# Holding DMA additions into weights back behind the first norm's factors and the constants

## The chip, the cores and the metric

The kernel runs on one core of a Trainium2 chip. The metric is the time of one execution on the device in microseconds (us). Before the change it was run three times: 941.42, 941.53 and 942.64 us, with a median of 941.53 us. One further execution was profiled. All durations of single instructions below come from that one.

## The reference

The model is an encoder trunk of two layers on 256 tokens with 1024 features each. Everything is float32. A layer has three parts, each with a norm ahead of it:

```python
for l in range(DEPTH):                                   # 2 layers
    x = x + 0.5 * swiglu(rms_norm(x, ffn1_norm[l]), ffn1_w_gate[l], ffn1_w_up[l], ffn1_w_down[l])
    h = rms_norm(x, mix_norm[l])
    proj = h @ w_in[l]                                   # queries, keys and values of two kinds of attention
    ...
    x = x + concat(out_a, out_b) @ w_out[l]
    x = x + 0.5 * swiglu(rms_norm(x, ffn2_norm[l]), ffn2_w_gate[l], ffn2_w_up[l], ffn2_w_down[l])
return rms_norm(x, final_norm)

rms_norm(x, g) = x * rsqrt(mean(x * x) + 1e-6) * g
swiglu(h, ...) = (silu(h @ w_gate) * (h @ w_up)) @ w_down     # hidden width 2816
```

So there are four feed-forward blocks (ffn) and two mixers, six norms ahead of them and a last one. All weights come from the chip's main memory, once.

## The kernel before

**Products.** Each float32 operand is split in two parts: ACT casts it to the matmul's rounded type (`act.copy`), and DVE subtracts that from the original. A product is then three matmuls: high by high, low by high, high by low. For a weight this means that a raw tile is loaded by DMA, and each half of it (j = 0, 1) costs one ACT cast and one DVE subtraction of 128x1024, which write two tiles (hi and lo) that PE reads.

**The list of weights.** `specs` is a list of steps in the order of use. An ffn has six column groups: group 0 is specs 0 to 3 (gate and up, two halves of the 1024 input features each), group 1 is specs 4 to 9 (four for gate and up, two for the down projection of the group before). In groups 2, 3 and 4 (`SEVEN`) the four block products of gate and up are made out of seven products in place of eight. This needs sums of weight blocks, and `seven()` makes them. It loads four raw tiles, here a, b, d and c; for group 2 they are specs 10, 11, 12 and 13. Two of the sums are made by the DMA engines: a DMA on POOL's queue that adds a block of w_up, read from main memory, onto a raw tile that already lies on the chip (`accum_op=ALU.add`). This is a "DMA addition". One adds block c onto raw tile b as soon as b's own load has been issued (`behind`). The other adds block b onto raw tile a once a has been split (`prep`). There are two such additions in each of three groups of four ffns, 24 in all. The remaining sums are DVE additions (`plus`).

**The planner.** `ahead(n)` runs while the program is written, not on the chip. It emits loads (on SP's queue), preparations and splits in the order of the list, as far as the number of raw tiles (`N_RAW` = 6) and the lookahead allow. A spec's split n is 2 * spec + j. It is called at each use of a weight (`weights()`), and where the second half of a weight is first read (`Split.part`).

**Holding back.** `issue(add)` appends a DMA addition to `pending`, and emits it at once unless `hold[0]` is true. `flush()` sets `hold[0]` to false and emits what is pending. `hold[0]` is set to true near the end of each ffn (`ffn_end`) and at the mixer's output projection. `Norm.stats()` flushes.

**The norms.** A norm's square sums are made by ACT. `stats()` (line 381) then sums them on DVE (`ms`), raises them to the power -1/2 on POOL (`r`), flushes, and halves r on DVE (`hr`). The factor r isn't multiplied into the activations: ACT's SiLU reads a finished gate product from PSUM with r as its scale (`tmp<-ps,r`), and DVE multiplies the up product by hr (`s<-ps,hr,tmp`), which gives the hidden tile. PE later transposes that tile (`ps<-ident,s`) for the down projection.

**The first stage.** `take_x` takes in x and the first weights by hand. `take_x(0)` and `take_x(1)` transpose x and split specs 0 and 1; between the calls PE makes the products of the first 512 features. `take_x(2)` (line 442) finishes the first two splits, which drops their raw tiles, calls `ahead(7)`, takes the last squares, calls `stats()`, and then `constants()` (line 469). `constants()` puts on POOL: eight small DMAs (gains, sink logits, the vectors of lambda), an iota, twelve memsets, four copies, a negation, and two products of lambda's vectors. Behind it PE makes the second half of gate and the second half of up, 24 matmuls each, and then starts on group 1's gate.

**Banks and order.** PSUM has eight banks. The ffn's output takes four; gate and up of one group take the other four, so the next group's gate writes into banks that the SiLUs of this one read first. Outside the middle of the mixer, each engine runs its instructions in the order in which the program gives them (`keep_in_program_order`); between engines, semaphores order them. An engine runs its own list strictly in that order: what stands behind a waiting instruction waits too. POOL's list holds both its own arithmetic and the issue of its DMAs. In the middle of the mixer a scheduler orders the instructions by times that it works out.

Of the kernel before, what the change touches and what calls it, by code (L numbers as in the profile page):

```python
# [34 lines left out]
def trunk(ctx: ExitStack, tc: tile.TileContext, x, n1, g1, u1, d1, nm, w_in, sink,  # L35
# [44 lines left out]
    def tmp(tag="tmp", bufs=5, shape=(P, 2, 256), dt=F32):  # L80
        return tp.tile(list(shape), dt, tag=tag, bufs=bufs, name=nm_(tag))
# [76 lines left out]
            issue(s.behind)  # L158


    pending, hold = [], [False]

    def issue(add):
        pending.append(add)
# [3 lines left out]
    def flush():  # L168
        hold[0] = False
        while pending:  # L170
            pending.pop(0)()
# [53 lines left out]
    def ahead(n):  # L225

        n = min(n, 2 * len(specs) - 1)
        while True:
            if at["split"] <= n and at["prep"] > at["split"] // 2:
                for _ in emit_split(*divmod(at["split"], 2)):  # L230
                    pass
                at["split"] += 1
            elif at["prep"] <= min(n // 2 + 1, len(specs) - 1) and at["dma"] > at["prep"] and \
                    (specs[at["prep"]].prep is None or at["split"] >= 2 * at["prep"]):
                if specs[at["prep"]].prep is not None:
                    specs[at["prep"]].prep()
                at["prep"] += 1
            elif at["dma"] < min(at["use"] + AHEAD, len(specs)) and (specs[at["dma"]].moves is None or len(raws) < N_RAW):
                if specs[at["dma"]].moves is not None:
                    for _ in emit_dma(at["dma"]):  # L240
                        pass
                at["dma"] += 1
            else:
                break
# [58 lines left out]
    class Norm:  # L303
# [77 lines left out]
        def stats(self, n=512):  # L381
            ms = tmp("ms", 2, (P, 2))
            dve.tensor_reduce(ms, self.ss.rearrange("p t (h q) -> p t h q", q=n // 256)[:, :, :, 0],
                              axis=mybir.AxisListType.X, op=ALU.add)
            dve.tensor_scalar(ms, ms, 1.0 / D, EPS, op0=ALU.mult, op1=ALU.add)
            self.r = tmp("r", 2, (P, 2))
            pool.tensor_tensor(self.r, ms, mhalf[:, 0:2], op=ALU.pow)
            flush()
            self.hr = tmp("hr", 2, (P, 2))
            dve.tensor_scalar_mul(self.hr, self.r, 0.5)  # L390

# [32 lines left out]
    def take_x(k):  # L424

        g, u = early
        if k == 0:
            for j in (0, 1):
                sl = norm.turn(j)
                next(g)  # L430
                norm.operands(j, sl)
                next(u)
        elif k == 1:
            for e in (g, u, g, u):
                next(e)
            norm.squares(0, 0, 512)
            norm.pair(2)
            norm.squares(1, 0, 512)
            ahead(5)
            norm.pair(3)  # L440
            norm.squares(0, 512, 512)
        elif k == 2:
            for e in early:
                next(e, None)
            ahead(7)
            norm.squares(1, 512, 512)
            norm.stats()
            constants()

    grow = const.tile([NG - 16, P], F32, name="grow")  # L450
    distB = const.tile([P, 2, S], F32, name="distB")
# [17 lines left out]
    def constants():  # L469
        for i, g in enumerate((nm, n2)):  # L470
            pool.dma_start(grow[i * 16:(i + 1) * 16], g.rearrange("l (k p) -> (l k) p", p=P))
        pool.dma_start(grow[32:34], subln)
        pool.dma_start(snk_in, sink.rearrange("l h -> (l h)").partition_broadcast(P))
        for i, a in enumerate((lq1, lk1, lq2, lk2)):
            pool.dma_start(lin[:, i], a.rearrange("l d -> (l d)").partition_broadcast(P))
        pool.iota(dist_i.rearrange("p a b -> p (a b)"), pattern=[[P, 2], [-1, S]], base=0, channel_multiplier=1)

        for c in range(4):
            pool.memset(qscA[0:64, c:c + 1], -0.125 / slopeA[c])
            pool.memset(qscA[64:128, c:c + 1], -0.125 / slopeA[c + 4])  # L480
            pool.memset(qscB[:, c:c + 1], -0.125 / slopeB[c])

        sv = snk_in.rearrange("p (l s c) -> p l c s", l=DEPTH, s=2)
        for t in range(2):
            for l in range(DEPTH):
                pool.tensor_copy(snk[:, l, :, t, :], sv[:, l])
        pool.tensor_scalar(nsnk.rearrange("p a b c d -> p (a b c d)"), snk.rearrange("p a b c d -> p (a b c d)"),
                           -1.0, 0.0, op0=ALU.mult, op1=ALU.add)
        for i in range(2):
            pool.tensor_tensor(lpr[:, i], lin[:, 2 * i], lin[:, 2 * i + 1], op=ALU.mult)  # L490
# [68 lines left out]
    class Residual:  # L559
# [14 lines left out]
        def late(self, k):  # L574

            if k == 1:
                self.nxt.pair(2)
                self.nxt.pair(3)
                self.squares(1)
            elif k == 2:  # L580
                self.nxt.stats()

    def ffn(norm, aside=None, before=None, final=False):
        def silu(out_, acc, t):
# [30 lines left out]
        def by_seven(h, g):  # L615
# [18 lines left out]
            p5 = prod(norm.summed(0), weights())  # L634
            late = g == max(SEVEN)
            p6 = prod(norm.summed(1), weights(look[0] - 5 if late else 0, late))
            u2 = put(flat(), p6, m1, ALU.subtract)
            u3 = put(m7, m7, u2, ALU.add)
            p4 = prod(norm.quarter(1, 1), weights(look[0] - 4 if late else 0, late))
            g1 = put(m1, p4, u3, ALU.subtract)  # L640
            w = weights(look[0] - 3 if late else 0)
# [372 lines left out]
    for l in range(DEPTH):  # L1014
        final = l == DEPTH - 1
        parts = ffn(norm, attention_constants, take_x) if l == 0 else ffn(norm)
        norm_m = Norm(16 + l * 8, False)
        ffn_close(parts, norm_m)
        norm2 = Norm(32 + l * 8)
        mix(l, norm_m, norm2)  # L1020
        parts = ffn(norm2, final_gain if final else None, final=final)
        if not final:
            norm = Norm((l + 1) * 8)
            ffn_close(parts, norm)
# [75 lines left out]
```

## Time and profile before

| | |
|---|---|
| median of three runs | 941.53 us |
| profiled execution, its own time | 942.09 us |
| its span (first to last instruction) | 940.3 us |
| mean granted TensorE clock | 0.992 |
| PE busy | 915.9 us, 97% |
| DVE busy | 760.7 us, 81% |
| ACT busy | 569.0 us, 61% |
| POOL busy | 57.8 us, 6% |
| mean DMA rate | 207 GB/s |

Times in the timelines are microseconds from the start of the span. A row of a timeline gives the start, the duration, the engine, the line, the operation, what it writes and reads by the names of the program's tiles (without numbers), how many instructions are merged in the row (x), and in brackets the idle time of the engine just before it with what ended it. Almost all instructions are issued through a helper at line 50, so the tile names tell them apart: `w` and `raw` are weights, `ps` a bank of PSUM, `r` and `hr` the norm's factors, `tmp` and `s` activations. SPq and POOLq are the queues on which DMAs are issued. A DMA row gives its size and the time from issue to landing.

### The profile page before, as it was taken

To read this page: it belongs to the slowest core of one execution; us is meant where nothing else is said; L and a number is where in the kernel's file an instruction comes from. 1 tells how busy PE (TensorE), PEld (TensorE's weight loads), DVE (VectorE), ACT (ScalarE), POOL (GpSimd) and SP (SyncE) were. 2 spreads that over 40 slices of the span, in tenths; PEclk is the share of its full clock that TensorE was granted. 3 is DMA by queue.
4 is the path that set the end of the run, shared out by engine and by line. 5 is a ranking of instruction groups with operands and counts; after the bars stand their busy time and mean duration, and the time that the engine had idled before them with its cause. 6 is when DMAs were issued, how large, how long until landed. Compare 5 with 4: busy or idle time off the path is not lost.

```text
span 940.3 us, 12548 instructions
## 1 busy us (share of the span) xinstructions
PE 915.9 (97%) x4732; PEld 772.9 (82%) x4732; DVE 760.7 (81%) x1074; ACT 569.0 (61%) x893; POOL 57.8 (6%) x77
## 2 busy tenths in 40 slices
PE   7499999999999999999999999999999999999997
PEld 6388888889988888888888888888998788888886
DVE  6376999977986668999875799996798566799994
ACT  7464766656765565675665566665577476465561
POOL 0220110000010000010000010000000001001011
PEclk9799999999999999999999999999999999999999
DMA  9893987966425875897858687978373467597731
GB/s 340 274 240 99 295 257 213 307 182 166 149 91 179 231 217 154 250 264 248 291 166 247 166 250 191 274 258 241 102 229 105 149 203 204 143 300 205 229 127 46
DMA packets 110893, 194.58 MB, mean 207 GB/s; under 512 B 3566, under 2 KB 31280, under 8 KB 110832
## 3 DMA queue, kind: packets, MB, share of 16 engines
q1 hardware_dynamic: 96528, 166.74, 52.1%
q0 software_dynamic: 12928, 25.46, 15.5%
q10 hardware_dynamic: 1376, 1.57, 0.5%
q8 instruction: 37, 0.61, 0.3%
q14 instruction: 24, 0.20, 0.1%
HBM read 192.71 MB, written 1.05 MB: 206 GB/s over the span
## 4 chain that ended last, share of the span: by engine, by line
PE 82%; DVE 10%; DMA 4%; issue 2%; ACT 2%; POOL 0%; POOLq 0%; ACTq 0%; DVEq 0%
PE ps L50 82%; DVE w L50 6%; DMA raw<-in_ffn_w_up_dram 3%; DVE tmp L50 2%; DVE raw L50 1%; ACT w L50 1%; DVE s L50 1%; DMA xk<-in_x_dram 1%; ACT s L50 0%; ACT tmp L50 0%; POOL raw L50 0%; ACT junk L50 0%; POOL r L50 0%; DVE xk L50 0%; POOLq L1095 0%
## 5 line engine op out<-in xcount | busy, mean ns | idle before, releaser
L50 PE MATMUL ps<-w,s 128*128 128x512 f32 (+1 forms) x2754 | 642.0, 391 | 12.5 <-ACT tmp L50 12.1
L50 PEld LDWEIGHTS ps<-w,s 128*128 128x128 f32 x2754 | 513.2, 189 | 118.6 <-ACT tmp L50 13.3
L50 DVE TENSOR_TENSOR w<-raw,w 128x1024 fp32r<-128x1024 f32 (+1 forms) x440 | 460.9, 1094 | 57.0 <-ACT w L50 55.8
L50 ACT CAST w<-raw 128x1024 fp32r<-128x1024 f32 (+1 forms) x440 | 390.9, 948 | 83.0 <-DVE raw L50 70.5
L50 PE MATMUL ps<-w,q 128*128 128x512 f32 x432 | 101.9, 389 | 0.0
L50 PEld LDWEIGHTS ps<-w,q 128*128 128x128 f32 x432 | 81.1, 188 | 16.8
L50 PE MATMUL ps<-s,w 128*128 128x256 f32 x672 | 84.0, 285 | 0.0
L50 PEld LDWEIGHTS ps<-s,w 128*128 128x128 f32 x672 | 81.7, 191 | 1.1
L50 ACT ACTIVATE s<-ps,gcol 128x256 fp32r<-128x256 f32 (+1 forms) x80 | 31.4, 488 | 44.2 <-PE ps L50 42.6
L50 DVE TENSOR_TENSOR raw<-raw,raw 128x1024 f32<-128x1024 f32 x48 | 56.4, 1216 | 0.0
L50 POOL DMA_DIRECT2D raw<-in_ffn_w_up_dram x24 | 31.3, 1303 | 387.1 <-DVE w L50 160.2
L50 ACT CAST s<-ps 128x512 fp32r<-128x512 f32 x44 | 23.9, 593 | 41.1 <-PE ps L50 41.1
L50 DVE TENSOR_TENSOR s<-ps,s 128x512 fp32r<-128x512 f32 x44 | 28.4, 683 | 21.4 <-ACT s L50 21.4
L50 PE MATMUL ps<-ident,s 128*128 128x128 f32 x304 | 40.3, 274 | 0.3 <-DVE s L50 0.3
L50 PEld LDWEIGHTS ps<-ident,s 128*128 128x128 f32 x304 | 35.0, 140 | 6.3 <-DVE s L50 0.9
L50 ACT ACTIVATE tmp<-tmp,r 128x512 f32<-128x512 f32 x24 | 17.3, 721 | 34.1 <-DVE tmp L50 34.1
L50 ACT ACTIVATE s<-s,negm 128x256 f32<-128x256 f32 x64 | 31.9, 500 | 6.6 <-DVE negm L50 6.4
L50 ACT COPY tmp<-ps 128x512 f32<-128x512 f32 x28 | 16.4, 585 | 30.6 <-PE ps L50 29.3
L50 PE MATMUL ps<-w,v 128*128 128x512 f32 x144 | 34.6, 389 | 0.0
L50 ACT CAST q<-tmp 128x512 fp32r<-128x512 f32 x20 | 12.4, 621 | 35.0 <-DVE tmp L50 34.9
L50 PEld LDWEIGHTS ps<-w,v 128*128 128x128 f32 x144 | 27.0, 188 | 5.6
L50 ACT ACTIVATE tmp<-ps,r 128x512 f32<-128x512 f32 (+1 forms) x24 | 14.3, 642 | 26.3 <-POOL r L50 13.4
(106 smaller groups left out, 426.9 us busy)
## 6 DMA issues: line engine op xcount, KB each, us to landing
raw<-in_ffn_w_down_dram SPq DMA_DIRECT2D x44, 1024.0 KB, 5.8
raw<-in_ffn_w_gate_dram SPq DMA_DIRECT2D x39, 1024.0 KB, 5.7
raw<-in_ffn_w_up_dram SPq DMA_DIRECT2D x39, 1024.0 KB, 5.6
raw<-in_ffn_w_up_dram POOLq DMA_DIRECT2D x24, 1024.0 KB, 10.1
raw<-in_w_in_dram SPq DMA_DIRECT2D x14, 1024.0 KB, 5.8
raw<-in_ffn_w_gate_dram SPq DMA_DIRECT2D x8, 512.0 KB, 6.4
raw<-in_ffn_w_up_dram SPq DMA_DIRECT2D x8, 512.0 KB, 7.4
raw<-in_w_in_dram SPq DMA_DIRECT2D x8, 512.0 KB, 6.0
```

Of the source, the lines that this page charges most:

```text
L50: ins = issue(*a, **k)
```

## The change

There are three edits. `hold[0]` starts as true, so DMA additions are kept from the first stage on. `stats()` no longer flushes. Its two callers flush instead: `take_x(2)` behind `constants()`, and `Residual.late(2)`, which serves all later norms, right behind `stats()`, that is, behind `hr`.

```diff
-    pending, hold = [], [False]
+    pending, hold = [], [True]
 
     def issue(add):
         pending.append(add)
...
             self.r = tmp("r", 2, (P, 2))
             pool.tensor_tensor(self.r, ms, mhalf[:, 0:2], op=ALU.pow)
-            flush()
             self.hr = tmp("hr", 2, (P, 2))
             dve.tensor_scalar_mul(self.hr, self.r, 0.5)
...
             norm.squares(1, 512, 512)
             norm.stats()
             constants()
+            flush()
...
             elif k == 2:
                 self.nxt.stats()
+                flush()
```

## The prediction

> **What bounds the kernel now.** I read the page first, then PE's waits, then the timelines of the engines around the one wait that stands out.
>
> ```profile
> span 940.3 us, 12548 instructions
> PE 915.9 (97%) x4732; PEld 772.9 (82%) x4732; DVE 760.7 (81%) x1074; ACT 569.0 (61%) x893; POOL 57.8 (6%) x77
> PE   7499999999999999999999999999999999999997
> PEclk9799999999999999999999999999999999999999
> ```
>
> TensorE is busy 97% of the span, so only PE's own idle time is to be had. Its second slice (23.5 to 47 us) is the only poor one after the start: busy 4 tenths, clock 7 tenths. The waits of PE over the whole run show where it went (the two rows left out are the first loads of the inputs):
>
> ```profile
> PE ps L50 <- ACT tmp L50: 12.1, 1, 12.1
> ...
> PE ps L50 <- DVE w L50: 0.4, 1, 0.4
> PE ps L50 <- DVE s L50: 0.3, 1, 0.3
> ```
>
> One wait of 12.1 us is about half of PE's idle time (940.3 - 915.9 = 24.4). It is for ACT. The timelines follow it back, PE, ACT, DVE, POOL in this order (start, us, then the instructions, and in brackets the idle time ahead of them and its releaser):
>
> ```profile
> 14.96 16.61 PE L50 MATMUL ps<-w,s 128*128 128x512 f32 x72
> 43.71 7.53 PE L50 MATMUL ps<-w,s 128*128 128x512 f32 x24 [12.14 <-ACT tmp L50]
> 51.08 1.03 PE L50 MATMUL ps<-ident,s 128*128 128x128 f32 x8
> 51.87 30.18 PE L50 MATMUL ps<-w,s 128*128 128x512 f32 x132
> 81.89 2.89 PE L50 MATMUL ps<-w,q 128*128 128x512 f32 x12
> ...
> 28.29 1.28 ACT L50 ACT_TABLE_LOAD   x1
> 42.97 1.26 ACT L50 ACTIVATE tmp<-ps,r 128x512 f32<-128x512 f32 x2 [13.39 <-POOL r L50]
> 44.12 3.89 ACT L50 CAST w<-raw 128x1024 fp32r<-128x1024 f32 x4
> 64.80 2.00 ACT L50 CAST w<-raw 128x1024 fp32r<-128x1024 f32 x2
> ...
> 27.46 0.17 DVE L50 TENSOR_SCALAR ms<-ms 128x2 f32<-128x2 f32 x1
> 47.60 1.40 DVE L50 SCALAR_TENSOR_TENSOR s<-ps,hr,tmp 128x512 f32<-128x512 f32 x2
> ...
> 40.68 1.48 POOL L50 DMA_DIRECT2D raw<-in_ffn_w_up_dram  x1 [39.18 <-DMA raw<-in_ffn_w_up_dram]
> 41.69 1.25 POOL L50 TENSOR_TENSOR r<-ms,mhalf 128x2 f32<-128x2 f32 x1
> 42.39 1.08 POOL L50 DMA_DIRECT2D grow<-in_mix_norm_dram  x1
> 45.62 1.02 POOL L50 DMA_DIRECT2D s<-in_lam_q_dram  x1
> 49.26 0.54 POOL L50 DMA_DIRECT2D s<-in_lam_k_dram  x1 [2.62 <-DMA raw<-in_ffn_w_up_dram]
> ```
>
> The sum of squares is ready at 27.46 + 0.17 = 27.63. The power that makes r of it runs only at 41.69: POOL stood 39.18 us at the DMA addition issued before it, whose target is a load of w_up that was still under way. ACT's SiLUs waited 13.39 for r. PE finished its 96 gate and up products at 14.96 + 16.61 = 31.57 and needs a bank that the two SiLUs free.
>
> **The change part by part.**
>
> *The first stage: the first addition goes behind the norm's factors and the constants.* The planner emits it in `ahead(7)` of `take_x(2)`: by then the first two raw tiles are popped, specs 10 and 11 are loaded (11 has a `behind`), and `stats()` follows. With `hold` true it is kept, and only this one, since specs 0 to 9 have no addition. `flush()` then issues it behind `constants()`; from there on `hold` is false as before.
>
> The gain in r: the power can start at 27.71 (0.08 behind the sum, as in a later norm: 314.25 + 0.17 to 314.50, rows below) and takes 1.25 at most, so r is there by 28.96. ACT's table load ends at 28.29 + 1.28 = 29.57, so the SiLUs run from 29.6 and the first ends at 30.3 (0.7 later, half of 1.26 and a little). That is before 31.57: PE's wait of 12.14 goes to zero, with 1.3 us to spare.
>
> What is late next: the transposes after those 24 products need the hidden tile. Before, it was done at 47.60 + 1.40 = 49.00, which is 6.03 behind the first SiLU; that makes 35.6, and PE wants it at 31.57 + 24 products. The loads behind the casts in between:
>
> ```profile
> 19.32 3.79 SPq L152 DMA_DIRECT2D raw<-in_ffn_w_down_dram  x2
> raw<-in_ffn_w_down_dram SPq DMA_DIRECT2D x1, 1024.0 KB, 12.7
> raw<-in_ffn_w_up_dram SPq DMA_DIRECT2D x1, 1024.0 KB, 12.6
> 27.38 1.15 SPq L152 DMA_DIRECT2D raw<-in_ffn_w_up_dram  x1
> 43.71:47.50 3.79, 3.79 (x9) 3.05 (x10) 3.79 (x4) 3.79 (x5) 2.93 (x6) 0.50 1.10 200
> 51.08:57.00 5.92, 5.92 (x32) 5.05 (x31) 1.79 (x4) 5.29 (x12) 1.68 (x13) 1.00 0.92 244
> ```
>
> The third and fourth of ACT's four casts read spec 8, landed at 19.32 + 12.7 = 32.0; they are reached at 30.8 + 1.9 = 32.7. So the loads are just ahead of the work there.
>
> The second gain is in the clock. The windows' last three columns are clock, DMA share and GB/s: after the wait PE ran at 0.50 for 3.79 us, then at 1.00. The 24 products took 51.08 - 43.71 = 7.37; at the rate of the later 132, (81.89 - 51.87) / 132 = 0.2274 each, they take 5.46. Without the pause these 1.91 are saved too. The Trainium skill (TensorE: Matmul & The Clock Gate, "The HAM clock gate") gives half the clock after an idle window of about 3.4 us and the full one after as long a busy stretch, which would be up to 1.7 us here and a time of 927.7; the trace's 1.91 is used. PE's next need, the transposes, is then at 31.57 + 5.46 = 37.0, and the hidden tile (35.6) is still in time, by 1.4.
>
> *What the held addition costs.* On POOL it now stands behind eight DMA issues, an iota, twelve memsets, four copies, a negation and two products, and the products wait for their vectors (the landing rows below, the shortest and the longest among them):
>
> ```profile
> grow<-in_diff_subln_dram POOLq DMA_DIRECT2D x1, 1.0 KB, 6.1
> s<-in_lam_k_dram POOLq DMA_DIRECT2D x1, 64.0 KB, 10.1
> raw<-in_ffn_w_up_dram SPq DMA_DIRECT2D x1, 1024.0 KB, 14.1
> raw<-in_ffn_w_up_dram POOLq DMA_DIRECT2D x1, 1024.0 KB, 8.3
> raw<-in_ffn_w_up_dram POOLq DMA_DIRECT2D x24, 1024.0 KB, 10.1
> raw<-in_ffn_w_up_dram POOLq DMA_DIRECT2D x1, 1024.0 KB, 13.2
> ...
> 82.14 0.59 ACT L50 COPY tmp<-ps 128x512 f32<-128x512 f32 x1 [5.18 <-PE ps L50]
> 59.44 0.53 POOL L50 TENSOR_TENSOR s<-s 128x128 f32<-128x128 f32 x1 [2.93 <-DMA s<-in_lam_k_dram]
> ```
>
> The first constant's DMA follows the power's start by 42.39 - 41.69 = 0.70: 28.41. The seventh follows by 45.62 - 42.39 = 3.23: 31.64. The eighth comes 0.54 later, 32.18; before, it stood until the addition landed (40.68 + 8.3 = 49.0 against 49.26), which is gone. It lands after 10.1, at 42.3; a product of 0.53, and the addition is issued at 42.9, against 40.68 before. Bounds: with 6.1 the constants are there at 38.3, and the addition waits for its target as before (27.38 + 12.6 = 40.0), so 40.7; with 14.1, the longest landing of a load in that stretch, 46.9. It lands 8.3 to 13.2 later: from 49.0 to 60.1; with the median 10.1, at 53.0.
>
> Who waits: the two casts of spec 11, ACT's row at 64.80 (a spec of this size has two casts; the four at 44.12 are specs 7 and 8, and 9 and 10 lie between). Shifted by 14.05 they are due at 50.75, so ACT may stand for 2.3 us, between 0 and 9.4. Behind them on ACT are casts and the copies for the sums, on DVE the hidden tile of the next group, wanted by PE's transposes behind its 12 products at 81.89. The cover is the idle time before ACT's copy at 82.14: 5.2 us of delay cost nothing, 9.4 would cost 4.2. I take 0, as 2.3 lies well inside. The next addition, into spec 10's tile, stays behind this one; it is issued behind the split of spec 10, by 50.8 or behind the first, lands by 64.0 with 13.2, and its reader comes behind ACT's copy at 82.14 - 14.05 = 68.1. The constants are first read in `attention_constants`, at the end of this ffn, and they come earlier than before.
>
> The Trainium skill (DMA: Bandwidth & Descriptors, "Queues, rings and completion order") says that each DMA engine goes round the queues in turn by packets. By that the constants, on POOL's queue, need not wait for the weights queued on SP's, and with the page's fixed 2.0 us they would land near 34, the addition would go at 40.7, and the sum would be the same; the 10.1 us of the trace say that the landing is slower than that.
>
> *Later stages: the flush follows hr instead of r.*
>
> ```profile
> 314.25 0.17 DVE L50 TENSOR_SCALAR ms<-ms 128x2 f32<-128x2 f32 x1
> 314.50 0.69 POOL L50 TENSOR_TENSOR r<-ms,mhalf 128x2 f32<-128x2 f32 x1 [38.92 <-DVE ms L50]
> 321.10 1.33 POOL L50 DMA_DIRECT2D raw<-in_ffn_w_up_dram  x1 [5.90 <-ACT w L50]
> ```
>
> hr is an instruction of DVE and the additions are POOL's; on POOL the order stays power, additions, and there the addition waits 5.90 us for something else. 0 us in all five later norms.
>
> *The sum.* -12.14 - 1.91 = -14.05, against the profiled execution's 942.09 us (span 940.3): 928.04. The median of the runs is 941.53, 0.56 lower: **927.5**. Behind 43.71 PE waits for 0.4 and 0.3 us only (its waits above), so the rest moves up as a block.
>
> **The rivals.**
>
> *The addition comes too late, by more than the cover.* For: the bound of 60.1, and a DMA share of 0.92 to 1.10 in this stretch. Against: the middle value leaves 2.9 us of cover. Cost up to 4.2, plus 1.91 if PE pauses long enough to lose its clock: 928.5 to 933.6; say 930.5.
>
> *A shorter wait stays.* The bank or the hidden tile is late by 1 to 3 us, since the weights' loads become due at the very time at which they land (32.0 against 32.7). A clock that stays low for a while in any case would belong here (1.91). 928.5 to 930.5; say 929.5.
>
> *Slower.* The constants' small packets get no turn while SP's loads keep the engines full. The casts of spec 11 then hold ACT and DVE, and PE stops at the next hidden tile. It decides from the point where the delay exceeds cover and gain, 5.2 + 14.05: the addition landed at 70.0, issued at 57 to 62, the vectors 24 us or more on their way. For a landing at 60: addition at 60.6, landed at 73.8 with 13.2, delay 23.1, loss 17.9 + 1.9, net +5.8: 947.3. Against: the longest landing here is 14.1, and 10.1 was measured with loads queued beside it.
>
> *It does nothing.* If r were late for another reason than the addition (the row names w_up's load only for the addition, not for r), PE would still wait: 941.5. Against: r starts 1.01 us behind the addition, after 14 us with its input ready.
>
> **How the numbers follow.** My forecast has 0.76, the late addition 0.10, the shorter wait 0.08, slower 0.03, nothing 0.03. 0.2% is 1.9 us, about what a measurement of this kernel can tell from no change. All but the last two are faster: 0.94; same 0.03, slower 0.03. The forecast's own spread is a microsecond or two: the middle part of the mixer is put in order by a planner's times and may fall out slightly otherwise. The range reaches up into the first two rivals, to 931.0, and down to 925.8, for a little more of PE's remaining waits.
>
> **What would show it.** The power of the first norm at about 27.7 us on POOL, the constants' DMAs behind it, the addition at about 43 behind the second product; PE's 24 products starting at 31.6 at a full clock; no wait of PE over 1 us behind the start; ACT's casts of spec 11 at 51 to 54, named as waiting for a DMA. A wait of PE near 37 or near 70 to 75, or a DVE that runs behind until the end of this stage, would prove the sum wrong.

## The result, and the profile after

The changed kernel takes 928.61 us (median of four runs, 928.19 to 928.88), against 942.09 for the kernel before beside it: a ratio of 0.9856, with a 95% interval of 0.9839 to 0.9873. That is 13.5 us saved where 14.05 were forecast. The page of the changed kernel:

```profile
span 927.1 us, 12551 instructions
PE 915.0 (99%) x4732; PEld 771.7 (83%) x4732; DVE 761.1 (82%) x1074; ACT 569.3 (61%) x893; POOL 58.9 (6%) x77
PE   8999999999999999999999999999999999999997
PEclk9999999999999999999999999999999999999999
```

PE's waits in it (total, times, longest; the first loads left out):

```profile
...
PE ps L50 <- ACT tmp L50: 0.6, 1, 0.6
PE ps L50 <- DVE w L50: 0.5, 1, 0.5
PE ps L50 <- DVE s L50: 0.5, 2, 0.3
```

PE is busy for nearly the same time (915.0 us against 915.9), in a span that is 13.2 us shorter. The wait of 12.1 us is down to 0.6, and the second slice has its full clock. The timelines of the changed kernel, PE, ACT, POOL:

```profile
14.65 16.58 PE L50 MATMUL ps<-w,s 128*128 128x512 f32 x72
31.82 5.78 PE L50 MATMUL ps<-w,s 128*128 128x512 f32 x24 [0.59 <-ACT tmp L50]
37.44 1.04 PE L50 MATMUL ps<-ident,s 128*128 128x128 f32 x8
68.28 2.89 PE L50 MATMUL ps<-w,q 128*128 128x512 f32 x12
...
27.77 2.00 ACT L50 CAST w<-raw 128x1024 fp32r<-128x1024 f32 x2 [1.34 <-DMA raw<-in_ffn_w_up_dram]
29.79 1.28 ACT L50 ACT_TABLE_LOAD   x1
31.08 1.27 ACT L50 ACTIVATE tmp<-ps,r 128x512 f32<-128x512 f32 x2
58.26 2.00 ACT L50 CAST w<-raw 128x1024 fp32r<-128x1024 f32 x2 [6.99 <-DMA raw<-in_ffn_w_up_dram]
...
27.68 0.72 POOL L50 TENSOR_TENSOR r<-ms,mhalf 128x2 f32<-128x2 f32 x1 [26.18 <-DVE ms L50]
28.35 0.75 POOL L50 DMA_DIRECT2D grow<-in_mix_norm_dram  x1
39.97 0.47 POOL L50 TENSOR_TENSOR s<-s 128x128 f32<-128x128 f32 x1 [1.52 <-DMA s<-in_lam_k_dram]
44.85 1.38 POOL L50 DMA_DIRECT2D raw<-in_ffn_w_up_dram  x1 [4.42 <-ACT tmp L50]
```

Three of its landings (the load of the addition's target, the last vector of lambda, the addition; the last number is us from issue to landing):

```profile
raw<-in_ffn_w_up_dram SPq DMA_DIRECT2D x1, 1024.0 KB, 17.0
s<-in_lam_k_dram POOLq DMA_DIRECT2D x1, 64.0 KB, 7.6
raw<-in_ffn_w_up_dram POOLq DMA_DIRECT2D x1, 1024.0 KB, 13.3
```

The power for r runs at 27.68, right behind its input, the constants' DMAs follow it, and the addition goes out at 44.85. PE begins group 1 at 31.82, where it began at 43.71 before. But ACT now stands for 6.99 us at the casts of spec 11, which read the tile that the addition completes.

### The profile page after: what moved, and what is told of

It reads as the page before. It is cut to its first block, busy times and chain, and to the rows that moved or that the text cites. A ratio compares the mean times of both kernels' runs of the same rounds, so it can differ in the third digit from the quotient of the medians.

```text
span 927.1 us, 12551 instructions
## 1 busy us (share of the span) xinstructions
PE 915.0 (99%) x4732; PEld 771.7 (83%) x4732; DVE 761.1 (82%) x1074; ACT 569.3 (61%) x893; POOL 58.9 (6%) x77
## 3 DMA queue, kind: packets, MB, share of 16 engines
HBM read 192.71 MB, written 1.05 MB: 209 GB/s over the span
## 4 chain that ended last, share of the span: by engine, by line
PE 86%; DVE 6%; DMA 5%; issue 2%; ACT 1%; POOLq 0%; ACTq 0%; POOL 0%; DVEq 0%
PE ps L50 86%; DVE w L50 4%; DMA raw<-in_ffn_w_up_dram 3%; DVE tmp L50 1%; ACT w L50 1%; DVE raw L50 1%; DMA raw<-in_ffn_w_gate_dram 1%; DMA xk<-in_x_dram 0%; DVE s L50 0%; ACT tmp L50 0%; ACT s L50 0%; DVE xk L50 0%; ACT L50 0%; POOLq L1096 0%; ACTq L50 0%
## 5 line engine op out<-in xcount | busy, mean ns | idle before, releaser
L50 ACT ACTIVATE s<-ps,gcol 128x256 fp32r<-128x256 f32 (+1 forms) x80 | 31.5, 488 | 44.3 <-PE ps L50 42.7
L50 DVE SCALAR_TENSOR_TENSOR s<-ps,gcol,s 128x256 fp32r<-128x256 f32 x48 | 20.3, 477 | 11.9 <-ACT s L50 11.8
```

Source lines behind the costliest of these rows:

```text
L50: ins = issue(*a, **k)
```

## The experiments

**One part at a time.** The first kernel has only the first stage's part: `hold` starts as true, and `stats()` flushes as before, except when `take_x` calls it. The rest of its edit, against the kernel before:

```diff
-            flush()
+            if go:
+                flush()
...
-            norm.stats()
+            norm.stats(go=False)
             constants()
+            flush()
```

> Only the first stage's part of the change: the first addition goes behind the first norm's factors and the constants; in the later norms the flush stays between r and hr. My theory (the whole gain is the first norm's power no longer standing behind the addition on POOL): the same time as the changed kernel, 928.6 us within 0.5, PE's wait for ACT at 31 us under 1 us. Rival (part of the gain comes from the later stages, where hr no longer follows the additions): slower than the changed kernel by its part, over 0.5 us.

The second has only the later stages' part: the changed kernel with `hold` false at the start.

```diff
-    pending, hold = [], [True]
+    pending, hold = [], [False]
```

> Only the later stages' part: additions go out at once in the first stage, and in the later norms behind hr. My theory: the time of before, 942.1 us within 0.5, with PE's wait of 12 us in place. Rival (the later stages give a part of the gain): faster than before by more than 0.5 us.

The first took 929.79 us (929.35 to 930.25), beside 928.87 for the changed kernel. The second took 942.39, beside 942.49 for the kernel before: a ratio of 1.0004, 0.9995 to 1.0013. PE's longest wait in the second, and its POOL:

```profile
PE ps L50 <- ACT tmp L50: 12.6, 1, 12.6
...
40.79 1.48 POOL L50 DMA_DIRECT2D raw<-in_ffn_w_up_dram  x1 [39.29 <-DMA raw<-in_ffn_w_up_dram]
41.80 1.25 POOL L50 TENSOR_TENSOR r<-ms,mhalf 128x2 f32<-128x2 f32 x1
```

The stall is untouched, so the later part alone does nothing. The 0.9 us by which the first part came out slower than the whole was more than the 0.5 expected. Both were repeated later, together with a kernel that adds the later part to the next experiment:

> The first stage's part alone, once more. If the later part is worth nothing: within 0.5 us of the changed kernel beside it. If it is worth 0.9: 0.9 slower again.

> The changed kernel beside these: 928.7 us within 0.5. The addition lands at 58 us again and ACT waits for it 7 to 8 us, with PE waiting some tenths for DVE's hidden tile near 132 us, if the delay of the addition is what sets the end of the first stage.

> As the kernel that holds the first addition back behind r alone, but in the later norms the flush stands behind hr as in the changed kernel. The first-stage part alone came out 0.9 us slower than the whole change, though the later part alone changed nothing. Theory (the later part is worth nothing, and the 0.9 is spread between builds or runs): the same as the kernel without it, within 0.5 us. Rival (the later part is worth about 0.9 us once the first stage is quick): faster by 0.5 to 1.2 us.

The first part took 928.13 (927.87 to 930.45), the whole change 929.21 (928.31 to 929.59). The sign turned round, so what differs between them is the spread of about 1 us that each of these kernels shows from run to run. With the later part added, the next experiment's kernel took 927.73 (927.55 to 929.22), without it 928.19 (927.0 to 929.26). The later part is worth nothing that these runs can tell.

**Behind r, but ahead of the constants.** The kernel before with one edit: `hold` is true at the start, and `stats()` flushes right behind r, as it did.

```diff
-    pending, hold = [], [False]
+    pending, hold = [], [True]
```

> The first addition goes behind r but ahead of the constants (held back from the start, flushed in the norm right behind r as before). My theory: PE's wait at 31 us goes as in the changed kernel, since only r has to be ahead of the addition. The addition goes out as soon as its target has landed, at 40 to 41 us against 44.85, since the constants' DMAs no longer run beside the target's load; ACT's wait of 7.0 us for it falls under 2 us. Time 928.0 to 928.6 us, at most 0.6 better than the changed kernel. Rival (the constants ahead of the addition matter for the gain, since they are out of the way early): slower than the changed kernel by 0.5 us or more.

> The changed kernel once more beside the others, for comparison on the same chip: 928.6 us within 0.5 by every theory. If the waits of ACT for spec 6's load (1.34 us) and for the addition (7.0 us) are chance, they differ here by microseconds; if they follow from the change, they come again.

> The kernel that holds the first addition back behind r alone (ahead of the constants), once more: 927.2 us within 0.5.

It took 927.18 us (926.83 to 927.48) beside 928.87 for the changed kernel, and 928.19 beside 929.21 the second time, when the ranges overlapped and the first part alone, which also has the constants ahead, took 928.13. By the medians it is 1.0 to 1.7 us quicker than the change under study, where I had expected 0.6 at most: the gain needs r ahead of the addition, and the constants ahead of it seem to cost about 1 us, which the losses in the table further below bear out. Its timeline (POOL, ACT), and the landings of the load of the addition's target and of the addition:

```profile
26.99 0.72 POOL L50 TENSOR_TENSOR r<-ms,mhalf 128x2 f32<-128x2 f32 x1 [25.49 <-DVE ms L50]
41.10 1.50 POOL L50 DMA_DIRECT2D raw<-in_ffn_w_up_dram  x1 [13.39 <-DMA raw<-in_ffn_w_up_dram]
55.80 2.00 ACT L50 CAST w<-raw 128x1024 fp32r<-128x1024 f32 x2 [5.35 <-DMA raw<-in_ffn_w_up_dram]
...
raw<-in_ffn_w_up_dram SPq DMA_DIRECT2D x1, 1024.0 KB, 13.9
raw<-in_ffn_w_up_dram POOLq DMA_DIRECT2D x1, 1024.0 KB, 14.6
```

Its windows (the last three columns are clock, DMA share, GB/s):

```profile
31.00:36.60 5.60, 5.57 (x24) 4.56 (x25) 4.07 (x5) 4.34 (x5) 0.00 (x0) 1.00 1.05 387
36.60:41.00 4.40, 4.40 (x25) 3.78 (x24) 3.07 (x4) 3.75 (x10) 0.00 (x0) 1.00 1.05 384
```

The same windows of the changed kernel beside it, and there the issue of its addition and the casts that read it:

```profile
31.00:36.60 5.60, 5.60 (x25) 4.60 (x26) 4.13 (x5) 4.28 (x5) 4.18 (x22) 1.00 1.05 332
36.60:40.50 3.90, 3.90 (x23) 3.38 (x22) 3.02 (x4) 3.33 (x9) 0.52 (x2) 1.00 0.93 240
...
43.84 1.38 POOL L50 DMA_DIRECT2D raw<-in_ffn_w_up_dram  x1 [2.94 <-ACT tmp L50]
58.37 2.00 ACT L50 CAST w<-raw 128x1024 fp32r<-128x1024 f32 x2 [8.00 <-DMA raw<-in_ffn_w_up_dram]
```

With the constants' small DMAs beside the loads, the DMA engines are nearly as busy (a share of 1.05 and 0.93 in place of 1.05 twice) but move 332 and 240 GB/s in place of 387 and 384. The load of the addition's target finishes later for it, and the addition starts 2.7 to 3.8 us later (43.84 in this profile of the changed kernel and 44.85 in the first, against 41.10). Its reader starts later too: 58.37 against 55.80. I had expected ACT's wait to fall under 2 us; it fell only to 5.35, in the repeat to 3.21, and with the later part added to 5.04, because the addition itself takes 13.5 to 14.6 us from issue to landing there. One more thing differs: in the changed kernel the second addition goes out at 49.41 (50.32 in the first profile), while the first is still under way, and behind r alone only at 61.71, since POOL waits 9.60 us for the first addition before its last constant's DMA. How much of the changed kernel's wait is due to the two additions at once isn't shown.

**r made late.** The last kernel with two, and with six, POOL operations between the sum of squares and the first r. They work on a tile that is written over later.

```diff
+            if slow:
+                wait_on(ms, slow)
             pool.tensor_tensor(self.r, ms, mhalf[:, 0:2], op=ALU.pow)
...
+    def wait_on(ms, n):
+        flat = distB.rearrange("p a b -> p (a b)")
+        pool.memset(flat, 1.0)
+        pool.tensor_copy(flat[:, 0:2], ms)
+        for _ in range(n):
+            pool.tensor_scalar(flat, flat, 0.5, 0.25, op0=ALU.mult, op1=ALU.add)
```

> As the kernel that holds the first addition back behind r alone, with two POOL operations of 128x512 (about 1.8 us each, estimated as half of the 3.61 us that one of 128x1024 took) put between the sum of squares and the first r, on a tile that is written later in any case. They make r about 3.7 us late, at 32, while the addition still waits for its target until 41. PE should pause about 2 us at 31 us. My theory (a pause costs its length, and the clock falls only behind a long one): 1 to 2.5 us slower than without, clock 0.95 or more in the 4 us behind the pause. Rival (a short pause costs the clock too): 3 to 4.5 us slower.

> The same with six such operations: r about 11 us late, at 39 to 40, PE's pause about 9 us. My theory: the pause plus about 1.9 us of half clock, 10 to 11.5 us slower than the kernel without them, 938 to 939, and the first matmuls behind the pause again at a clock of about 0.5. Rival (the low clock behind the pause of before came from something else, the DMA additions or the constants then running): the pause alone, 9 us, and a full clock.

The operations took 0.69 us each, not 1.8, so both delays were short. With two of them r was still in time and PE didn't pause: 928.55 us, which tells nothing of the clock. With six PE paused for 2.1 us, and the time was 931.27 (929.35 to 933.78). PE's timeline:

```profile
32.99 7.35 PE L50 MATMUL ps<-w,s 128*128 128x512 f32 x24 [2.08 <-ACT tmp L50]
40.17 1.03 PE L50 MATMUL ps<-ident,s 128*128 128x128 f32 x8
```

Its windows at the pause and behind it:

```profile
30.90:32.99 2.09, 0.01 (x2) 0.01 (x1) 0.74 (x2) 0.74 (x2) 1.30 (x2) 1.00 1.05 386
32.99:36.50 3.51, 3.51 (x9) 2.77 (x10) 3.51 (x4) 3.51 (x5) 0.00 (x0) 0.57 1.05 387
```

The landing of its third addition, and behind it that in the kernel without the operations:

```profile
raw<-in_ffn_w_up_dram POOLq DMA_DIRECT2D x1, 1024.0 KB, 14.0
```

```profile
raw<-in_ffn_w_up_dram POOLq DMA_DIRECT2D x1, 1024.0 KB, 10.2
```

The 24 products took 40.17 - 32.99 = 7.18 us, 1.72 over the 5.46 at a full clock. So the half clock does belong to the pause, and not to the additions or constants, which go out only from 40.80 on here. But my theory that a short pause leaves the clock alone fell: in this profile 2.1 us of pause cost nearly as much clock as 12.1 did (1.91). Pause and clock make 3.8 us, against 2.7 by the medians beside the kernel with two operations, and 3.1 to 4.1 beside the earlier runs without any. The profiled run was the slowest, 2 to 3 us beyond that: its third addition took 3.8 us longer to land, and ACT waited 5.1 us for it; why that landing differs stays open.

**The addition made late.** The changed kernel with eight, and with twenty, such operations between the constants and the addition.

```diff
             constants()
+            wait_on(8)
             flush()
```

> As the changed kernel, with eight POOL operations of 128x512 put between the constants and the first addition (14 to 15 us in all): r is in time, but the addition goes out at about 55 us against 44 and lands at 66 to 69 against 58. If the idle time of ACT and DVE behind its reader (5.2 us) is used up already by the changed kernel's 7 to 8 us of wait, nearly all of the further delay shows: 7 to 11 us slower than the changed kernel, 936 to 940, with PE waiting for DVE at 70 to 75 us or later in the first stage. If there is more cover than that: under 4 us slower. Both ways it stays faster than before.

> As the changed kernel, with twenty POOL operations of 128x512 between the constants and the first addition (eight took 8.73 us and moved the addition's issue to 50.35 and its landing only to 59.8, so twenty should move the issue to 62 to 64 and the landing to 71 to 77). By the prediction's rule the loss begins 5.2 us behind 50.75 and then grows one for one, and the change is lost where the addition lands at 70: for a landing at 71 to 77, 942 to 949, with PE waiting 10 us or more for ACT or DVE at 70 to 85 us. Rival (the cover is far larger, since the delay is taken up by idle time later in the first stage too): 930 to 938.

They took 929.77 us (929.23 to 931.0) and 938.73 us (938.41 to 939.79). With eight the milder of the two expectations held. With twenty the time fell between the two: the addition landed at about 69, not at 71 to 77, and the cover is longer than the 5.2 us that I used, as shown below. The timeline with eight (POOL, ACT), then with twenty (POOL, PE, ACT):

```profile
41.67 8.73 POOL L50 TENSOR_SCALAR distB<-distB 128x512 f32<-128x512 f32 x8
50.35 2.72 POOL L50 DMA_DIRECT2D raw<-in_ffn_w_up_dram  x2
59.77 2.00 ACT L50 CAST w<-raw 128x1024 fp32r<-128x1024 f32 x2 [7.04 <-DMA raw<-in_ffn_w_up_dram]
```

```profile
60.44 2.72 POOL L50 DMA_DIRECT2D raw<-in_ffn_w_up_dram  x2
37.73 30.18 PE L50 MATMUL ps<-w,s 128*128 128x512 f32 x132
74.01 5.77 PE L50 MATMUL ps<-w,q 128*128 128x512 f32 x12 [6.09 <-ACT q L50]
69.27 1.99 ACT L50 CAST w<-raw 128x1024 fp32r<-128x1024 f32 x2 [15.98 <-DMA raw<-in_ffn_w_up_dram]
```

With eight, the addition went out 6.5 us later than in the changed kernel beside the third experiment (43.84), but its reader started only 1.4 later (59.77 against 58.37), since the addition landed in 9.3 us and not in 14.4. In the changed kernel the DMA engines are full from its issue to its landing (a share of 1.09 from 43.8 to 58.3 us). That an early addition there only shares them is my reading and not shown by itself; behind r alone, where the second addition isn't beside it, an issue 2.7 us earlier did bring the reader forward by 2.6. With twenty the addition went out at 60.44 and the delay showed.

These runs give the price of the delay. Let T be the start of PE's 12 products behind the row of 132 (81.89 before, 68.28 after). Where the last column group of the first ffn begins (the end of the stage, in what follows), PE waits for a DVE subtraction; the rows of that wait stand below for before, the changed kernel, the changed kernel again, the one behind r alone, and those with eight and twenty operations, with T's row ahead where it isn't shown yet. The casts of spec 11 are in the rows above and, for before, in the prediction.

```profile
164.52 13.45 PE L50 MATMUL ps<-w,s 128*128 128x512 f32 x58 [0.39 <-DVE w L50]
```

```profile
151.46 13.44 PE L50 MATMUL ps<-w,s 128*128 128x512 f32 x58 [0.53 <-DVE w L50]
```

```profile
67.34 2.89 PE L50 MATMUL ps<-w,q 128*128 128x512 f32 x12
151.59 13.49 PE L50 MATMUL ps<-w,s 128*128 128x512 f32 x58 [0.52 <-DVE w L50]
```

```profile
67.42 2.89 PE L50 MATMUL ps<-w,q 128*128 128x512 f32 x12
150.07 13.49 PE L50 MATMUL ps<-w,s 128*128 128x512 f32 x58 [0.41 <-DVE w L50]
```

```profile
67.60 2.89 PE L50 MATMUL ps<-w,q 128*128 128x512 f32 x12
152.96 13.45 PE L50 MATMUL ps<-w,s 128*128 128x512 f32 x58 [0.52 <-DVE w L50]
```

```profile
162.45 13.45 PE L50 MATMUL ps<-w,s 128*128 128x512 f32 x58 [0.52 <-DVE w L50]
```

| kernel | casts of spec 11, from T | T to the end of that wait | loss: over before's 82.63 |
|---|---|---|---|
| before | -17.09 | 82.63 | 0 |
| behind r alone | -11.62 | 82.65 | 0.02 |
| changed | -10.02 | 83.18 | 0.55 |
| changed, again | -8.97 | 84.25 | 1.62 |
| eight operations | -7.83 | 85.36 | 2.73 |
| twenty operations (T due at 37.73 + 30.02) | +1.52 | 94.70 | 12.07 |

In the last four the loss minus the second column is 10.57, 10.59, 10.56 and 10.55. So a delay is free up to T - 10.57, which is 17.09 - 10.57 = 6.5 us of cover, and beyond that each microsecond costs one. The changed kernel's third profile (loss 1.98 us) and the repeat of the first part (1.73) lie on this line too, at 10.56 and 10.58. The first part's first profile doesn't fall on it as closely: its casts came at T - 9.05 and it lost 1.86, not 1.52. Two profiles lie off it altogether, since a later addition was late in them: with r late by six operations, and behind r alone with the later part added, the casts of spec 11 came inside the cover, but the third addition landed in 14.0 and 12.8 us, against 9.6 to 10.8 in the twelve other profiles, ACT waited 5.1 and 3.9 us for it, and 2.92 and 1.76 us were lost. Each was the slowest execution of its kernel.

## Why the prediction was right, and where it was off

*The gain in r* came as worked out: the power at 27.68 (27.71 forecast), PE's wait of 12.14 gone but for 0.59. The rest is there because ACT's casts of spec 6 waited 1.34 for their load, which put the table load and the SiLUs 1.5 us later than I had them. That used up the spare 1.3. In the same kernel's second profile the SiLUs ran at 30.23 and PE didn't wait, so this part is the loads' spread between runs. It is the second rival's mechanism, at 0.6 us.

*The clock*: the 24 products took 37.44 - 31.82 = 5.62 us, 1.75 less than the 7.37 of before (1.91 forecast). The long pause's loss of clock was real, and the experiment with r late makes the pause its cause. Nor does it take a pause as long as the rule that the prediction quotes for the clock: there 2.08 us was enough, in the one profile that shows it.

*What is late next*: PE got the hidden tile at 37.44 without waiting for it, with DVE done at 37.0. I had 35.6; the margin was 0.4 us and not 1.4, as the late SiLUs moved it too.

*Later stages*: nothing, as forecast, shown by the second experiment.

*What the held addition costs* is the step that failed in its size: I took 0 for it. It was worked out as landing at 53.0, with the constants setting its issue at 42.9 (the terms given there make 42.8). Lambda's vectors landed sooner than I had (7.6 us against 10.1), so the products were done at 40.4. Then the addition waited for its own target, whose load took 17.0 us against the 12.6 that I carried over from before. Behind r alone, without the constants beside it, that load took 13.9, so most of the difference is put down to the constants' DMAs; the rest may be the further loads that ACT and DVE now make room for earlier. (The row names ACT as the releaser; that SiLU runs at 43.80 to 45.1 and the addition doesn't need it, while the target's load ends at 27.28 + 17.0 = 44.3.) The addition then took 13.3 us, not 10.1. ACT waited 6.99 where I had 2.3. My cover of 5.2 was near the measured 6.5, so the overrun cost 0.55 us in this profile, and 1.62 and 1.98 in the two others.

*The sum*: at PE's row of 12 products the changed kernel is 81.89 - 68.28 = 13.61 us ahead, of which 0.34 is an earlier start of this run (products done at 31.23, not 31.57). At the end of the stage it is 13.06 ahead, at the end of the span 13.2. The first rival's mechanism was thus at work beside my forecast, at 0.6 to 2.0 us of a gain of 13.5. The terms close: 14.05 forecast, less 0.59 of pause that stayed, 0.16 of clock and 0.55 of delay, plus the 0.34, make 13.09.

*The rival on the slower side* was put to the test by the twenty operations. It was right in kind, and wrong in two places. PE stopped first at the sums' operand (ACT q, 6.09 us), not at the next hidden tile. And with the reader at 69.3 us the kernel is still 4.1 us faster than before beside it; by one for one the change would be lost at about 73.4, where I had 70.0.

## What to carry to other kernels

A DMA issue that must wait for its target stands in its engine's list like any other instruction; if the engine also makes something small that the busiest engine needs soon, put the small thing first, and look at PE's pause and at the slow clock behind it as one cost. When a stall goes, carry the loads' landing times over with care: the work that it held back now competes with them. And hold a thing back only behind what must precede it: here r, and not the constants, which was worth about 1 us.

## What was not expected of the hardware

- A pause of PE of 2.1 us was followed by 3.5 us at a clock of 0.57, a loss of 1.72 us, close to the 1.91 behind a pause of 12.1. One profile shows it. Behind the changed kernel's pause of 0.59 the granted clock was 1.00, and the 24 products took 5.62, about 0.16 over the full rate.
- With eight small DMAs, 0.3 MB in all, beside the loads, the rate was 332 and 240 GB/s in place of 387 and 384 for some 9 us. The share of the DMA engines stayed high for most of it; at the lowest, from 37 to 39 us, it was 0.76 at 137 GB/s, against 1.06 at 386 without them.
- The first DMA addition, 1 MB, took from 8.3 us (before) to 14.6 (behind r alone) from issue to landing, and the second 15.1 in the changed kernel, where both were under way at once. With eight operations ahead of it, an issue 6.5 us later made the start of its reader only 1.4 us later.
